# Order of products, weight sums and row finishing in the down half of a squared-ReLU MLP

## Chip, cores and metric

The kernel runs on one core of one Trainium2 chip. The metric is the device time of one execution in microseconds (us); three executions of the kernel before were timed and their median is taken. One further execution was recorded by the hardware profiler, and the times of single instructions come from that one.

A core has TensorE (PE, matrix products into the accumulation banks of PSUM), VectorE (DVE), ScalarE (ACT), GpSimd (POOL) and SyncE (SP, which issues most DMAs). Each engine works through its own list of instructions in order.

## What is computed

Two decoder layers on 1024 tokens of width 1024, float32 throughout: a latent attention mixer in layer 0, a gated linear recurrence (HGRN2) in layer 1, and after each of them an MLP.

```python
def sq_relu_mlp(h, w1, w2):
    a = jax.nn.relu(h @ w1)
    return (a * a) @ w2          # w1: 1024 x 4096, w2: 4096 x 1024

# per layer
a = rms_norm(h, norm_gains[layer, 2])
h = h + rms_norm(sq_relu_mlp(a, mlp_w1[layer], mlp_w2[layer]), norm_gains[layer, 3])
```

The change touches the second product, `(a * a) @ w2`, with the norm and the residual sum behind it.

## The kernel before

A float32 matrix is used as two parts, a rounded one and the rest. `split` (L76, L77) makes them: ACT copies the rounded part, DVE subtracts it from the source. `mm3` (L81 to L83) adds three partial products of such parts into one bank of PSUM.

`mlp_down` computes `(a * a) @ w2` by a scheme with seven block products in place of eight. Tokens, the 4096 hidden features and the 1024 outputs are each halved; the result has four blocks c11, c12, c21, c22. The left factors are the seven sums of blocks of activations that the up half has left in DRAM (`hsp[0]` to `hsp[6]`); they have the features on the partitions. The right factors are the blocks b11, b12, b21, b22 of the weights and four sums of them, which are made here on DVE from blocks that SP loads into tiles `s11`, `s12`, `s21`, `s22` (their digits are left out in the profile: all are `s`).

The features are taken in two passes, c = 0 and c = 1 (`NC = 2`). One pass has four pairs of 128-wide chunks (`qs`). A product goes over the four pairs; for each pair `factors` loads and splits the left part (`sparts`) and the right part (`right(q)`, then `parts`), and 24 matmuls follow, into four banks, one for each of the four 128-token tiles (`banks`). `more=True` goes on adding to what the banks hold. `gather` moves the four banks to SBUF after a product: ACT copies (L1002) at c = 0 where there is nothing to add to, otherwise DVE adds (L1004). The split parts live in five working tiles `w` (one in `G0`, four in `G`), two for each pair; raw loads pass through three staging tiles.

Before, a pass runs so, where X is a set of four banks from pool `PG` and Y one from `PM`:

- product 0 in X, gathered to `U`; product 1 added to it, gathered to c11
- product 4 in Y with t1 = b12 - b11 (L939, in place in `s11`), gathered to c22; product 2 with b22 added to it, gathered to c12; beside it `less22` (L1018) makes b21 - b22 in `s21`
- product 5 in X with t2 = b22 - t1 (L948, in a tile `s12`), added to `U` (so U holds products 0 and 5 of both passes in the end)
- at c = 1: for each of the first four token tiles c12 += U (L1029), `finish_rows`, c22 += U (L1031), U += c21 (L1032)
- product 6 in Y with t3 = b22 - b12 (L953, after a second load of b12), added to c22; product 3 with t4 (L957, the fifth sum) added to the same banks; at c = 0 copied to c21, at c = 1 added to U by `done`

`finish_rows` takes a finished tile of 128 rows: mean squares on ACT (L135), `rstd` on DVE and a power on POOL (L145), a multiplication by the gains `gpost` on 1024 columns (L199), a fused multiply-add with the residual rows `xt` (L200), a store by POOL, and in layer 0 a second norm for the next mixer (L204). `xt` is one tile in layer 0 and three in layer 1. The last four token tiles are finished by `done`, called from `by_tiles`, which goes through product 3 tile by tile: in layer 0 the last two pairs, in layer 1 all four, whose right parts have tiles of their own there (`wx`). Their residual rows come by `rows_in` into tiles that the weight sums no longer need. In layer 0 the finished rows are transposed on PE (`into_features`, L176) for the next mixer.

What runs when: the program is put in order ahead of time. A planner simulates the engines and on each of them takes, among the instructions that it holds to be ready, the one that stands first in the program. `keep_in_program_order` holds an instruction behind the one that was written just before it for the same engine; the weight sums on DVE and the weight loads on SP have it.

## Time and profile before

| what | us |
|---|---|
| median of 3 runs | 2400.32 |
| lowest and highest | 2399.58, 2401.26 |
| the profiled execution, device time | 2396.59 |
| its span | 2394.9 |
| ACT busy | 1170.9 |
| POOL busy | 355.5 |
| PE's mean granted clock | 0.987 |

Down stage of layer 0: about 830 to 1150 us in the span; of layer 1: about 2065 us to the end. In rows of the timeline the first number is the start and the second the duration; `x2` is two instructions merged, and brackets show how long the engine stood idle before and what ended that. In rows by stretch each engine has its busy time and its count of instructions; PEclk is the granted clock as a share of full speed. A matmul's recorded duration is longer than the step from one to the next, since they are pipelined.

### The profile page before, as it was taken

Reading aid. Unit: us, or ns where it says so; the run is one execution under the profiler, and the core shown is the slowest. Engines: PE = TensorE matmul, PEld = TensorE weight load, DVE = VectorE, ACT = ScalarE, POOL = GpSimd, SP = SyncE. Lnnn points to the kernel's source line nnn. Section 1 sums busy time; section 2 is a strip of 40 time slices with the busy share of each in tenths; the row PEclk is TensorE's granted clock in tenths of the full one; section 3 lists DMA queues with packets and bytes.
Section 4 is the critical chain, followed back from the end, with each engine's and each line's share of the span. In section 5 each row is a group of like instructions: output and inputs, shape, how many; then the busy total and the mean of one; then the engine's idle time right before and its main releaser. Section 6 shows DMA issues by size and latency. Waiting matters only on the chain. (4 is left out here: it accounts for less than half of the span.)

```text
span 2394.9 us, 30791 instructions
## 1 busy us (share of the span) xinstructions
PE 2285.7 (95%) x11487; PEld 1918.8 (80%) x11487; DVE 1616.4 (67%) x2311; ACT 1170.9 (49%) x1908; POOL 355.5 (15%) x718
## 2 busy tenths in 40 slices
PE   9999999988899999998899999999978999999996
PEld 8889998866688878886788888888766788888885
DVE  5657884477676557578765667756777767467578
ACT  5445654363344454433575546754453445443443
POOL 1300000121121200001332213221211212100002
PEclk9999999999999999999999999999999999999998
DMA  6000002485554584554612333222455545663743
GB/s 216 27 27 10 10 10 90 157 267 164 172 184 151 187 299 133 190 181 149 219 45 88 106 105 116 83 77 80 150 184 187 200 149 172 214 238 132 257 138 141
DMA packets 229540, 341.51 MB, mean 143 GB/s; under 512 B 16999, under 2 KB 136846, under 8 KB 229390
## 3 DMA queue, kind: packets, MB, share of 16 engines
q1 hardware_dynamic: 205582, 259.84, 33.7%
q0 software_dynamic: 23808, 79.71, 9.0%
q8 instruction: 90, 1.47, 0.3%
q14 instruction: 60, 0.49, 0.1%
HBM read 255.61 MB, written 83.89 MB: 142 GB/s over the span
## 5 line engine op out<-in xcount | busy, mean ns | idle before, releaser
L77 DVE TENSOR_TENSOR w<-raw,w 128x1024 fp32r<-128x1024 f32 (+1 forms) x256 | 280.7, 1102 | 175.9 <-ACT w L76 174.9
L76 ACT ACTIVATE w<-raw 128x1024 fp32r<-128x1024 f32 (+1 forms) x256 | 240.7, 947 | 248.0 <-PE mm L83 82.1
L81 PE MATMUL mm<-A,w 128*128 128x512 f32 x832 | 330.9, 400 | 30.5 <-ACT he L784 12.8
L82 PE MATMUL mm<-A,w 128*128 128x512 f32 x832 | 329.7, 397 | 0.6 <-DVE A L77 0.5
L83 PE MATMUL mm<-A,w 128*128 128x512 f32 x832 | 327.9, 396 | 0.5 <-DVE w L77 0.5
L76 ACT ACTIVATE w<-s 128x1024 fp32r<-128x1024 f32 x156 | 165.1, 1058 | 318.6 <-PE c L83 107.0
L77 DVE TENSOR_TENSOR w<-s,w 128x1024 fp32r<-128x1024 f32 x156 | 190.6, 1222 | 143.2 <-ACT w L76 142.7
L81 PEld LDWEIGHTS mm<-A,w 128*128 128x128 f32 x832 | 158.4, 191 | 72.5 <-ACT he L784 16.1
L145 POOL TENSOR_TENSOR rstd<-rstd,nhalf 128x1 f32<-128x1 f32 x56 | 56.3, 1008 | 964.9 <-DVE rstd L144 939.0
L83 PEld LDWEIGHTS mm<-A,w 128*128 128x128 f32 x832 | 158.7, 191 | 34.2 <-DVE w L77 1.0
L82 PEld LDWEIGHTS mm<-A,w 128*128 128x128 f32 x832 | 158.4, 190 | 33.0 <-DVE A L77 1.4
L82 PE MATMUL mm<-w,w 128*128 128x512 f32 x432 | 171.0, 396 | 12.2 <-DVE w L77 12.2
L781 POOL DMA_DIRECT2D hsp<-h x208 | 112.1, 540 | 467.2 <-ACT h L785 242.6
L83 PE MATMUL mm<-w,w 128*128 128x512 f32 x432 | 169.6, 394 | 0.0
L81 PE MATMUL mm<-w,w 128*128 128x512 f32 x432 | 154.9, 394 | 4.1 <-DVE y L1004 3.2
L81 PE MATMUL mm<-w,A 128*128 128x256 f32 (+2 forms) x352 | 111.1, 318 | 3.6 <-ACT A L76 3.4
L784 ACT ACTIVATE h<-h 128x512 f32<-128x512 f32 x96 | 60.2, 627 | 109.2 <-DVE h L825 70.9
L83 PE MATMUL mm<-w,A 128*128 128x256 f32 (+2 forms) x352 | 111.0, 317 | 0.0
L82 PE MATMUL mm<-w,A 128*128 128x256 f32 (+2 forms) x352 | 110.7, 316 | 0.0
L82 PEld LDWEIGHTS mm<-w,w 128*128 128x128 f32 x432 | 82.1, 190 | 31.2 <-DVE w L77 14.3
L81 PEld LDWEIGHTS mm<-w,w 128*128 128x128 f32 x432 | 81.4, 189 | 24.8 <-ACT w L76 5.7
L81 PE MATMUL c<-T,w 128*128 128x512 f32 x256 | 99.7, 390 | 1.6 <-DVE h L825 1.6
(415 smaller groups left out, 5705.0 us busy)
## 6 DMA issues: line engine op xcount, KB each, us to landing
raw<-in_mlp_w_dram SPq DMA_DIRECT2D x108, 512.0 KB, 4.2
hsp<-h POOLq DMA_DIRECT2D x208, 256.0 KB, 3.1
s<-in_mlp_w_dram SPq DMA_DIRECT2D x80, 512.0 KB, 5.5
raw<-hsp SPq DMA_DIRECT2D x76, 512.0 KB, 4.1
raw<-in_hgrn_w_in_dram SPq DMA_DIRECT2D x64, 512.0 KB, 4.1
sx<-hsp SPq DMA_DIRECT2D x36, 512.0 KB, 4.2
res<-xt POOLq DMA_DIRECT2D x20, 512.0 KB, 4.1
xt<-in_x_dram SPq DMA_DIRECT2D x16, 512.0 KB, 5.7
```

Of the source, the lines that this page charges most:

```text
L76: ACT.activation(dst[:, 0], src, AF.Copy)
L77: DVE.tensor_tensor(dst[:, 1], src, dst[:, 0].bitcast(F32), ALU.subtract)
L81: PE.matmul(ps, lhs[0], rhs[0], start=start, stop=False, skip_group_check=more)
L82: PE.matmul(ps, lhs[0], rhs[1], start=False, stop=False, skip_group_check=more)
L83: PE.matmul(ps, lhs[1], rhs[0], start=False, stop=stop, skip_group_check=more)
L145: POOL.tensor_tensor(r, r, nhalf[:, :1], ALU.pow)
L781: POOL.dma_start(hsp[i, p * P:(p + 1) * P, :], h)
L784: ACT.activation(h, src, AF.Relu)
```

## The change

- The sums are made in place, four for each pair: t1 as before; after product 2's factors `sums` makes t2 in `s11` and t4 in `s21` from it; t3 is made in `s22` beside product 5.
- At c = 1 `U` (product 0 of both passes) is added to c12, c22 and c21 right after product 1. The mean squares of c11 and the gains' multiplication of that half follow there; `finish_rows` gets the other half as `part` and its residual rows by `rows_in` in `s11` tiles.
- Products 5, 6 and 3 accumulate in one set of banks X: after product 5 it is added to c12, after 6 to c22, after 3 to c21. The two sets change pools at odd c.

```diff
-    def finish_rows(wp, y, ms, gpost, gpre, src, dst, t, xt_bufs=2, xt=None):
+    def finish_rows(wp, y, ms, gpost, gpre, src, dst, t, xt_bufs=2, xt=None, part=slice(0, D)):
...
-        DVE.tensor_tensor(y, y, gpost, ALU.mult)
+        DVE.tensor_tensor(y[:, part], y[:, part], gpost[:, part], ALU.mult)
...
-                def t2(q):
-                    t = new(wr, [P, 2, 512], F32, "s12", 3)
-                    tc.keep_in_program_order(DVE.tensor_tensor(t, s22[q], s11[q], ALU.subtract))
-                    return t
+                def sums(q):
+                    tc.keep_in_program_order(DVE.tensor_tensor(s11[q], s22[q], s11[q], ALU.subtract))
+                    tc.keep_in_program_order(DVE.tensor_tensor(s21[q], s21[q], s11[q], ALU.subtract))
                 def t3(q):
                     b12 = load12(q)
-                    tc.keep_in_program_order(DVE.tensor_tensor(b12, s22[q], b12, ALU.subtract))
-                    return b12
-                def t4(q):
-                    tc.keep_in_program_order(DVE.tensor_tensor(s21[q], s21[q], s11[q], ALU.add))
-                    return s21[q]
+                    tc.keep_in_program_order(DVE.tensor_tensor(s22[q], s22[q], b12, ALU.subtract))
...
+                first, second = [(PG, "mm"), (PG, "tr")], [(PM, "mm"), (PM, "c")]
+                if c % 2:
+                    first, second = second, first
+                X = four(*first)
                 product(0, X, first11)
                 gather(U, X)
                 product(1, X, load21, True)
                 gather(c11, X)
+                if last:
+                    for to in (c12, c22, c21):
+                        for t in range(4):
+                            DVE.tensor_tensor(to[t], to[t], U[t], ALU.add)
+                    gpost = row_bcast(wp, "gpost", norm_gains[layer, 3], D)
+                    ms11 = []
+                    for t in range(4):
+                        ms11.append(meansq(c11[t], new(wp, [P, 512], BF16, "junk"), new(wp, [P, 1], F32, f"ms{t}")))
+                        DVE.tensor_tensor(c11[t], c11[t], gpost[:, :512], ALU.mult)
+                Y = four(*second)
                 product(4, Y, t1)
                 gather(c22, Y)
-                def less22(q):
-                    tc.keep_in_program_order(DVE.tensor_tensor(s21[q], s21[q], s22[q], ALU.subtract))
-                product(2, Y, load22, True, less22)
+                product(2, Y, load22, True, sums)
                 gather(c12, Y)
-                X = four((PG, "mm"), (PG, "tr"))
-                product(5, X, t2)
-                gather(U, X, U)
+                X = four(*first)
+                product(5, X, s11.get, after=t3)
+                gather(c12, X, c12)
                 if last:
                     for t in range(4):
-                        DVE.tensor_tensor(c12[t], c12[t], U[t], ALU.add)
-                        finish_rows(wp, y[t], None, gpost, gpre, src, dst, t, xt_bufs=1 if gpre is not None else 3)
-                        DVE.tensor_tensor(c22[t], c22[t], U[t], ALU.add)
-                        DVE.tensor_tensor(U[t], U[t], c21[t], ALU.add)
-                Y = four((PM, "mm"), (PM, "c"))
-                product(6, Y, t3)
-                gather(c22, Y, c22)
+                        ms12 = meansq(c12[t], new(wp, [P, 512], BF16, "junk"))
+                        finish_rows(wp, y[t], [ms11[t], ms12], gpost, gpre, src, dst, t, xt=rows_in("s11", t),
+                                    part=slice(512, D))
+                product(6, X, s22.get, True)
+                gather(c22, X, c22)
                 if not last:
-                    product(3, Y, t4, True)
-                    gather(c21, Y)
+                    product(3, X, s21.get, True)
+                    gather(c21, X)
```

Behind this, `done` adds X to c21 in place of Y to U, and `by_tiles` takes `s21.get` and loads its residual rows into `s21` tiles.

More of the change, by code (lines that the diff above doesn't have):

```diff
@@ L997, in mlp_down, with rows_in @@
                     y += [new(wp, [P, D], F32, f"y{t}") for t in range(4, NT)]
+                def rows_in(tag, t):
+                    xt = new(wp, [P, 2, 512], F32, tag, KC // 2).rearrange("p a b -> p (a b)")
+                    tc.keep_in_program_order(SP.dma_start(xt, src[t * P:(t + 1) * P, :]))
+                    return xt
                 def gather(out, banks, base=None):
@@ L1033, in mlp_down @@
-                Y = four((PM, "mm"), (PM, "c"))
-                product(6, Y, t3)
-                gather(c22, Y, c22)
-                def rows_in(t):
-                    xt = new(wp, [P, 2, 512], F32, "s11", KC // 2).rearrange("p a b -> p (a b)")
-                    tc.keep_in_program_order(SP.dma_start(xt, src[t * P:(t + 1) * P, :]))
-                    return xt
+                        ms12 = meansq(c12[t], new(wp, [P, 512], BF16, "junk"))
+                        finish_rows(wp, y[t], [ms11[t], ms12], gpost, gpre, src, dst, t, xt=rows_in("s11", t),
+                                    part=slice(512, D))
@@ L1053, in done @@
                     def done(t):
-                        DVE.tensor_tensor(c21[t], Y[t], U[t], ALU.add)
+                        DVE.tensor_tensor(c21[t], X[t], c21[t], ALU.add)
                         finish_rows(wp, y[4 + t], None, gpost, gpre, src, dst, 4 + t, xt=xts[t])
                         POOL.dma_start(later[t * P:(t + 1) * P, :], y[4 + t])
-                    product(3, Y, t4, True, n1=2)
+                    product(3, X, s21.get, True, n1=2)
                     xts = []
-                    by_tiles(3, Y, t4, 2, done, False, lambda: xts.extend(rows_in(4 + t) for t in range(4)))
+                    by_tiles(3, X, s21.get, 2, done, False, lambda: xts.extend(rows_in("s21", 4 + t) for t in range(4)))
                 else:
@@ L1070, in done @@
                         xt = xts[t]
[L1071 removed]
+                        DVE.tensor_tensor(c21[t], X[t], c21[t], ALU.add)
                         ms = meansq(c21[t], new(wp, [P, 512], BF16, "junk"))
```

5 lines of the change are left out of this document (1 added, 4 removed).

## The prediction

> **What bounds the kernel now.** I read the page's busy line first, then busy time by stretch for each product of the down stage, then PE's timeline where the stretches are not full, and at last VectorE's own order there.
>
> ```profile
> PE 2285.7 (95%) x11487; PEld 1918.8 (80%) x11487; DVE 1616.4 (67%) x2311; ACT 1170.9 (49%) x1908; POOL 355.5 (15%) x718
> ```
>
> TensorE sets the time: it is busy for 95% of the span. An edit on VectorE (DVE) is worth something only where PE waits for DVE. A product of the down stage is 96 matmuls (4 pairs of weight chunks x 2 x 4 banks x 3 partial products), in the order 0, 1, 4, 2, 5, 6, 3, once for c = 0 and once for c = 1. These rows are layer 0, c = 1, products 1, 4, 2, 5, the first 21.8 us of 6 and its rest; then layer 1, the same two parts of 6.
>
> ```profile
> core 0: us, PE busy (x) PEld busy (x) DVE busy (x) ACT busy (x) POOL busy (x), PEclk, DMA share, GB/s
> 1005.20:1027.00 21.80, 21.80 (x98) 18.05 (x97) 13.25 (x13) 8.04 (x9) 0.00 (x0) 1.00 0.84 305
> 1027.00:1048.80 21.80, 21.80 (x97) 17.80 (x96) 15.19 (x16) 8.74 (x11) 0.00 (x0) 1.00 0.47 164
> 1048.80:1070.60 21.80, 21.80 (x97) 18.05 (x98) 16.87 (x17) 7.95 (x8) 0.00 (x0) 1.00 0.39 125
> 1070.60:1092.30 21.70, 21.70 (x98) 17.96 (x97) 16.62 (x18) 8.04 (x8) 0.00 (x0) 1.00 0.55 191
> 1092.30:1114.10 21.80, 17.00 (x67) 13.29 (x66) 21.34 (x27) 9.35 (x14) 7.21 (x2) 0.92 0.20 73
> 1114.10:1125.10 11.00, 7.86 (x39) 6.38 (x38) 8.26 (x11) 4.91 (x8) 2.57 (x3) 1.00 0.47 143
> 2328.20:2350.00 21.80, 15.63 (x61) 12.21 (x60) 21.80 (x31) 10.14 (x19) 8.53 (x5) 0.88 0.19 65
> 2350.00:2361.20 11.20, 9.53 (x38) 7.12 (x37) 11.20 (x12) 3.92 (x4) 1.60 (x3) 0.93 0.72 254
> ```
>
> Products 1 to 5 keep PE full, with DVE busy 13 to 17 of 21.8 us. In product 6 it turns over: DVE has no idle time (21.80 of 21.80) and PE drops to 15.63. So the last two products of c = 1 are bound by DVE, twice in the kernel, and nothing else of the down stage is. How much is lost there:
>
> ```profile
> 1086.82 0.62 PE L81 MATMUL mm<-w,w 128*128 128x512 f32 x2
> 1092.26 0.62 PE L81 MATMUL mm<-w,w 128*128 128x512 f32 x2
> 1109.29 0.80 PE L82 MATMUL mm<-w,w 128*128 128x512 f32 x1 [4.73 <-DVE w L77]
> 1120.92 1.03 PE L176 MATMUL tr<-ident,y 128*128 128x128 f32 x8
> 1125.13 0.47 PE L81 MATMUL mm<-w,w 128*128 128x512 f32 x1 [3.17 <-DVE y L1004]
> 1150.24 0.40 PE L83 MATMUL c<-w,w 128*128 128x512 f32 x1
> ...
> 2328.19 0.61 PE L81 MATMUL mm<-w,w 128*128 128x512 f32 x2
> 2346.61 0.80 PE L82 MATMUL mm<-w,w 128*128 128x512 f32 x1 [6.00 <-DVE w L77]
> 2347.21 0.63 PE L83 MATMUL mm<-w,w 128*128 128x512 f32 x1
> 2347.64 0.63 PE L82 MATMUL mm<-w,w 128*128 128x512 f32 x1
> 2355.88 0.50 PE L82 MATMUL mm<-w,w 128*128 128x512 f32 x1 [1.21 <-DVE w L77]
> 2361.17 0.47 PE L81 MATMUL mm<-wx,w 128*128 128x512 f32 x1 [0.46 <-DVE y L1004]
> 2382.83 0.39 PE L83 MATMUL c<-wx,w 128*128 128x512 f32 x1
> ```
>
> The first two rows are the starts of two neighbouring pairs of chunks: 24 matmuls in 5.44 us, 0.227 each, so 21.8 a product and 43.5 for products 6 and 3. Layer 1 takes from 2328.19 to 2383.06 (the last start plus one step), 54.9: **11.4 us lost**. Layer 0 takes from 1092.26 to 1150.47, 58.2, with three groups of 8 transposes in it (1.03 each): **11.6 us lost**. The waits are only part: after the 6.00 us wait matmuls step by 0.43 (2347.21 to 2347.64), the lower clock that PEclk 0.88 shows. With the waits this goes too.
>
> **What DVE does there.** Layer 1's group rows for 2328.2 to 2350, then single rows in order of time:
>
> ```profile
> L199 DVE TENSOR_TENSOR y<-y,gpost 128x1024 f32<-128x1024 f32 x4 | 4.9, 1215 | 0.0
> L1029 DVE TENSOR_TENSOR y<-y,u 128x512 f32<-128x512 f32 x4 | 2.7, 682 | 0.0
> ...
> 2327.50 1.28 DVE L1004 TENSOR_TENSOR u<-mm,u 128x512 f32<-128x512 f32 x2
> 2328.70 1.28 DVE L1004 TENSOR_TENSOR u<-tr,u 128x512 f32<-128x512 f32 x2
> 2344.21 1.21 DVE L199 TENSOR_TENSOR y<-y,gpost 128x1024 f32<-128x1024 f32 x1
> 2345.35 1.21 DVE L77 TENSOR_TENSOR w<-s,w 128x1024 fp32r<-128x1024 f32 x1
> ```
>
> Back to back, a 512-wide operation costs 0.60 us (two in 1.20) and a 1024-wide one 1.14. The split at 2345.35, the one that PE's 6.00 us wait ends on, stands behind 16 adds of 512 (four each at L1004, L1029, L1031, L1032) and four full multiplications (L199).
>
> **The change, summed for DVE.** Per product: 8 splits, 9.1; a set of 4 gathers, 2.4; 4 weight sums, 4.6.
>
> - Product 6 before: 9.1 + 2.4 + 12 adds (7.2) + 4.6 (t3) + per row a multiplication 1.14 and a fused step 1.2 (9.4) = 32.7, and a second fused step per row in layer 0 (4.8) = 37.5. Room: 21.8.
> - Product 6 after: the adds are in product 1, t3 is in product 5, half of each multiplication is in product 4. Left: 9.1 + 2.4 + 4 x (0.6 + 1.2) = 18.7; layer 0 23.5.
> - Product 3: 9.1 + 2.4 + 4.6 becomes 11.5; t4 is now made in product 2.
> - Product 1 gets 7.2 on 13.25, 20.4. Product 4 gets 2.4 on 15.19, 17.6. Product 2 gets a second sum, 4.6 on 16.87, 21.4. Product 5 has t3 where t2 was, 16.6.
>
> All of them fit but layer 0's product 6, 1.7 over, which the slack ahead of and behind it takes up. The five working weight tiles hold a product's split about one pair (5.44 us) ahead, which covers the fullest, product 2. If that cover is gone, a wait like layer 1's is the price, 11 us with its clock. I take 1 us for products 1 to 2 of both layers (0 to 22), and 2 us left in product 6 (0 to 11.6).
>
> The sums removed at c = 0 (one in five) are worth nothing there: PE had no wait in those products. Moved DMAs: `load12` goes from product 6 to 5 (DMA share 0.55, room), and the rows of `src` come through SP into `s11` tiles, behind the splits of product 5, which run a pair ahead of PE; behind them on SP stand the loads of product 6's left factors, whose tiles come free at the same pace. Below nothing, since layer 0's single `xt` tile goes: inside the 11.6. ACT has 8 to 10 of 21.8 in each stretch, so four earlier mean squares are free.
>
> **The new wait.** Product 6 must now accumulate in the banks that product 5's gather is still reading, four boundaries more (two layers, c = 0 and 1); PE's stream stands behind it. The nearest rows are the 6 to 3 boundary at c = 0, where this is so already, and all waits of this kind in the run:
>
> ```profile
> 960.99 0.39 PE L83 MATMUL c<-w,w 128*128 128x512 f32 x1
> 961.36 0.47 PE L81 MATMUL mm<-w,w 128*128 128x512 f32 x1
> ...
> PE mm L81 <- DVE y L1004: 3.6, 2, 3.2
> ```
>
> A step of 0.37 in place of 0.227: 0.14 lost. The two recorded waits (3.2 and 0.46) are those where DVE had a queue. I take 0.14 x 4 = 0.6 (up to 3.2 each, 12.8); the gather is ahead of product 6's splits in priority. A rule speaks against this edit: the Trainium skill, "Perfetto Trace Analysis", section "Matmuls", wants independent groups of matmuls rotated through different PSUM banks, so that an eviction overlaps the next group. By it the sum would carry four whole sets of gathers, 9.6 in place of 0.6. The row above does not bear it out where DVE is free: four banks in turn leave each gather some 2 us.
>
> **The first power on POOL.**
>
> ```profile
> 2339.02 7.95 POOL L145 TENSOR_TENSOR rstd<-rstd,nhalf 128x1 f32<-128x1 f32 x4 [262.21 <-DVE rstd L144]
> ```
>
> Four take 7.95 after 262 us of idle. It delays the fused steps to about 8 us into product 6, before and after; splits stand between them now as then. Cost 0, up to 5 if DVE's stream is blocked behind it.
>
> **The end of the span, and what follows layer 0.** Three rows of DVE at the end of layer 1, one of ACT after layer 0, and two waits of PE there:
>
> ```profile
> 2384.40 0.69 DVE L1071 TENSOR_TENSOR y<-c,u 128x512 f32<-128x512 f32 x1
> 2387.65 0.69 DVE L1073 TENSOR_TENSOR y<-y,gpost 128x512 f32<-128x512 f32 x1
> 2389.13 1.41 DVE L1077 SCALAR_TENSOR_TENSOR s<-y,rstd,s 128x512 f32<-128x512 f32 x2 [0.73 <-POOL rstd L145]
> ...
> 1189.54 1.06 ACT L76 ACTIVATE w<-raw 128x1024 fp32r<-128x1024 f32 x1 [4.70 <-DMA raw<-in_hgrn_w_in_dram]
> ...
> PE mm L81 <- ACT f L1122: 4.3, 1, 4.3
> PE mm L81 <- ACT A L76: 1.1, 1, 1.1
> ```
>
> The last row's multiplication waits from 2384.40 to 2387.65 behind other rows, because late sums (t4) made PE go by pairs, not by tiles, and three tiles ended together. With the sums ready the tiles end apart: up to 3.2 saved, I take 2 (0 to 3.2). After layer 0, PE waits 1.1 for the first rows' features, which now come earlier: I take 1 (0 to 1.1). The 4.3 us wait further on hangs on a load of the next mixer's weights (ACT's row at 1189.54, 4.70 for the DMA); I leave it, and keep 4 us either way for the range.
>
> **Sum.** -11.6 - 11.4 - 2 - 1 + 2 + 1 + 0.6 = -22.4. The profiled execution took 2396.59 (span 2394.9 and 1.7 around it), which gives 2374.2. It lies 3.7 under the median of the runs, 2400.32; I set the saving against the median and say **2378**.
>
> **Rivals.**
>
> - A, half: finishing work has priority over product 6's splits, and layer 0 is still 1.7 over; the order puts row steps ahead of the third pair's splits, and one wait of about 5 us with its slow clock stays in each layer. For it: 16 operations went ahead of a needed split before. Against: they are 8 short ones now. 2378 + 2 x 5.5 = 2389. Chance 0.20.
> - B, the banks: each of the four new boundaries costs its whole gather, 2.4, as in the rule above: 2378 + 9 = 2387. For: the 3.2 us wait. Against: the 0.14. Chance 0.06.
> - C, slower: DVE's queue moves to products 1 to 2 of c = 1, 59.4 of 65.4 us full. It decides once the work ahead of a needed split there passes 5.44 us: then each layer waits there as now in product 6 (11.5), and product 5's gather comes late behind it (3.2 and as much for the clock, 6.4 in all) while product 6's wait stays halved: +11.5 + 6.4 - 6 is 12 a layer on 2400.32, 2424. Chance 0.06.
> - D, it does not do what it says: the planner's order keeps the same operations ahead of the splits, or the next mixer's wait gives the gain back; within 0.2%, 2396 to 2405. Chance 0.08.
>
> The forecast has 0.60 (2371 to 2385). A measurement of this kernel tells about 0.2%, 5 us, from no change. Faster is forecast, A and B: 0.86; same 0.08; slower 0.06. The range, 2370 (all waits, 3.2, 1.1 and some of the 4.3 gone) to 2391 (A with 2 more), holds 0.86 by the cases, somewhat less at its ends.
>
> **What would show it.** Right: in both layers product 6 of c = 1 takes some 22 to 24 us at PEclk 1.00, DVE has idle time there, no split ends a PE wait over 1 us, products 1, 4 and 2 show DVE near 20 and PE full, and 5 to 6 steps by under 0.5. Wrong: a wait on L77 in product 6 (A), on L1004 at 5 to 6 (B), PE gaps in 1 to 2 (C), or as many lost microseconds behind the down stage as were won in it (D).

## The result and the profile after

| | us |
|---|---|
| predicted | 2378, range 2370 to 2391 |
| after, median of 4 runs | 2372.7 (2370.5 to 2374.67) |
| before, beside them, median of 4 | 2400.79 (2399.58 to 2405.72) |
| ratio, 95% interval | 0.9879 [0.9862, 0.9896] |
| after once more, in a second set of runs, median of 5 | 2375.27, ratio 0.9905 [0.9888, 0.9921] |
| the profiled execution of after | 2374.67, span 2373.0 (before 2396.59, span 2394.9) |

In this section the two profiled executions are compared, whose spans differ by 21.9 us. The milestones are starts of PE's matmuls in the timeline: the start of each layer's down stage, the start of product 6 at c = 1, the end of product 3 (last start plus one step of 0.23), the end of the span. The down stage of layer 1 starts at 2052.6 us in before and at 2045.6 in after.

| part, us | before | after | difference |
|---|---|---|---|
| up to the down stage of layer 0 | 826.1 | 828.0 | +1.9 |
| from there to product 6, c = 1 | 266.2 | 265.9 | -0.3 |
| products 6 and 3, layer 0 | 58.2 | 47.9 | **-10.3** |
| from there to the down stage of layer 1 | 902.1 | 903.8 | +1.7 |
| from there to product 6, c = 1 | 275.6 | 274.9 | -0.7 |
| products 6 and 3, layer 1 | 54.9 | 43.5 | **-11.4** |
| from there to the end | 11.8 | 9.0 | -2.8 |

The page's busy line shows PE with nearly the same work in a shorter span:

```profile
PE 2284.0 (96%) x11487; PEld 1923.2 (81%) x11487; DVE 1599.9 (67%) x2303; ACT 1171.8 (49%) x1909; POOL 344.2 (15%) x718
```

Busy time by stretch of after, columns as in the prediction. First layer 0, c = 1, products 1, 4, 2, 5, 6, 3 (six rows); then the same six products of layer 1.

```profile
1006.80:1028.50 21.70, 21.70 (x98) 17.96 (x97) 19.94 (x25) 7.94 (x8) 0.00 (x0) 1.00 0.70 252
1028.50:1050.30 21.80, 21.80 (x97) 17.85 (x96) 17.56 (x20) 10.91 (x17) 0.00 (x0) 1.00 0.75 253
1050.30:1072.10 21.80, 21.80 (x97) 17.87 (x97) 20.59 (x21) 7.96 (x8) 0.00 (x0) 1.00 0.57 192
1072.10:1093.80 21.70, 21.70 (x97) 17.98 (x96) 16.23 (x17) 8.77 (x10) 0.00 (x0) 1.00 0.64 199
1093.80:1118.00 24.20, 23.77 (x114) 19.59 (x112) 23.29 (x32) 16.74 (x26) 7.55 (x11) 1.00 0.42 149
1118.00:1141.80 23.80, 23.80 (x113) 19.64 (x114) 15.85 (x21) 10.29 (x17) 1.84 (x2) 1.00 0.48 155
...
2233.40:2255.20 21.80, 21.80 (x98) 18.06 (x97) 20.04 (x25) 8.04 (x9) 0.00 (x0) 1.00 0.71 254
2255.20:2276.90 21.70, 21.70 (x97) 17.75 (x96) 17.46 (x20) 10.82 (x17) 0.00 (x0) 1.00 0.70 246
2276.90:2298.70 21.80, 21.80 (x96) 17.88 (x97) 21.80 (x21) 12.04 (x12) 0.00 (x0) 1.00 0.50 169
2298.70:2320.50 21.80, 21.80 (x98) 18.04 (x97) 19.28 (x21) 9.15 (x11) 0.00 (x0) 1.00 0.67 223
2320.50:2342.20 21.70, 21.70 (x97) 18.00 (x96) 18.10 (x24) 9.65 (x16) 6.63 (x8) 1.00 0.54 187
2342.20:2364.00 21.80, 21.80 (x97) 17.84 (x96) 13.97 (x23) 5.98 (x14) 1.66 (x3) 1.00 0.38 149
```

PE is full in all of them, at clock 1.00, but for 0.43 us in layer 0. Layer 1's product 6 went from 15.63 of 21.8 at clock 0.88 to 21.70 of 21.70, and DVE has 3.6 us idle in it. Most of what layer 0 has over 21.8 there (24.2 and 23.8) is no loss: PE makes 32 transposes in between, some 0.13 us each (8 in 1.03); in before 24 of them stood in this stretch and 8 behind it.

PE's waits in the down stage, first all of layer 1's, then all of layer 0's (us in total, times, longest):

```profile
PE mm L81 <- ACT u L1006: 0.2, 1, 0.2
...
PE mm L81 <- ACT w L76: 0.5, 1, 0.5
PE mm L81 <- DVE y L1008: 0.4, 1, 0.4
PE mm L82 <- DVE w L77: 0.2, 1, 0.2
```

Of the waits for a split in product 6 (6.00 and 4.73 us before) nothing is left. The new wait for the banks is next, from PE's timeline: the last matmul of product 5 and the first of product 6 in layer 1, then the first of product 3 in layer 0 behind a group of transposes.

```profile
2320.25 0.39 PE L83 MATMUL c<-w,w 128*128 128x512 f32 x1
2320.48 0.39 PE L81 MATMUL mm<-w,w 128*128 128x512 f32 x1
...
1117.99 0.47 PE L81 MATMUL mm<-w,w 128*128 128x512 f32 x1 [0.43 <-DVE y L1008]
```

2320.25 to 2320.48 is the ordinary step, 0.23. The other three boundaries from 5 to 6 step by 0.23 as well. DVE's timeline shows why there is room: two gathers merged from 2318.64, the third from 2320.00, the fourth only from 2321.27, with a row step between them.

```profile
2318.64 1.37 DVE L1008 TENSOR_TENSOR y<-mm,y 128x512 f32<-128x512 f32 x2
2320.00 0.69 DVE L1008 TENSOR_TENSOR y<-c,y 128x512 f32<-128x512 f32 x1
...
2320.67 0.68 DVE L200 TENSOR_TENSOR y<-y,gpost 128x512 f32<-128x512 f32 x1
2321.27 0.68 DVE L1008 TENSOR_TENSOR y<-c,y 128x512 f32<-128x512 f32 x1
```

A gather of a bank has to be done only when PE comes to that bank again, and PE takes the four banks one after the other. The first bank's gather starts at 2318.64 while PE is still in the last two.

And the tail in layer 1, the last row's steps on DVE:

```profile
2364.20 0.69 DVE L1075 TENSOR_TENSOR y<-c,y 128x512 f32<-128x512 f32 x1 [0.56 <-PE c L83]
2365.74 0.69 DVE L1077 TENSOR_TENSOR y<-y,gpost 128x512 f32<-128x512 f32 x1 [0.85 <-ACT junk L135]
2367.22 1.41 DVE L1081 SCALAR_TENSOR_TENSOR s<-y,rstd,s 128x512 f32<-128x512 f32 x2 [0.73 <-POOL rstd L145]
```

From the add to the multiplication it takes 1.54 us now, 3.25 before: the row no longer stands behind others, and what is left of the idle time is its own chain (the mean square on ACT, the power on POOL). That is 1.7 of the 2.8 us. The other 1.1 lie ahead of the add: it starts 0.2 us behind the end of product 3 (2364.00) now and started 1.35 us behind it before (2383.05 to 2384.40).

### The profile page after: what moved, and what is told of

Read it like the earlier page. It is cut to its first block, busy times and chain, and to the rows that moved or that the text cites. A ratio compares the mean times of both kernels' runs of the same rounds, so it can differ in the third digit from the quotient of the medians.

```text
span 2373.0 us, 30769 instructions
## 1 busy us (share of the span) xinstructions
PE 2284.0 (96%) x11487; PEld 1923.2 (81%) x11487; DVE 1599.9 (67%) x2303; ACT 1171.8 (49%) x1909; POOL 344.2 (15%) x718
## 5 line engine op out<-in xcount | busy, mean ns | idle before, releaser
L145 POOL TENSOR_TENSOR rstd<-rstd,nhalf 128x1 f32<-128x1 f32 x56 | 45.1, 807 | 965.6 <-DVE rstd L144 942.2
L81 PE MATMUL c<-T,w 128*128 128x512 f32 x256 | 99.7, 390 | 1.5 <-DVE h L827 1.5
L82 PE MATMUL c<-T,w 128*128 128x512 f32 x256 | 99.6, 389 | 0.0
L83 PE MATMUL c<-T,w 128*128 128x512 f32 x256 | 98.8, 389 | 0.0
```

The source lines that it names most:

```text
L81: PE.matmul(ps, lhs[0], rhs[0], start=start, stop=False, skip_group_check=more)
L82: PE.matmul(ps, lhs[0], rhs[1], start=False, stop=False, skip_group_check=more)
L83: PE.matmul(ps, lhs[1], rhs[0], start=False, stop=stop, skip_group_check=more)
L145: POOL.tensor_tensor(r, r, nhalf[:, :1], ALU.pow)
```

## The experiments

Two parts of the change could have taken PE's waits away: the weight sums that are ready earlier, and the adds and multiplications that left product 6. The theory of the prediction is the load: PE waits when DVE has more to do in product 6 than there is room, whatever the work is. The rival is the chain: a weight sum made inside the product that uses it puts a further step on DVE ahead of the rounding on ACT and the split on DVE, and that is late even where there is room for the load. Besides, the banks (rival B), the 7.95 us power on POOL, and what lies between the two down stages had to be tested. For each run "stretch" means products 6 and 3 at c = 1, counted from 96 steps behind the first matmul of product 5, so that a delay within product 5 or at its end is in it too (counted from the first matmul of product 6 it is 0.10 to 0.15 us shorter in adds only, t3 late and idle sum, 2.0 us shorter in layer 1 of adds late, and the same in the others); without any wait it takes 43.5 us in layer 1 (192 steps of 0.2267), and in layer 0 that and some 0.13 us for each transpose in it.

| kernel | median, us (runs) | ratio to before [interval] | stretch, layer 0 (transposes in it) | between the down stages | stretch, layer 1 | tail |
|---|---|---|---|---|---|---|
| before | | 1 | 58.2 (24) | 902.1 | 54.9 | 11.8 |
| after | 2372.7 (4) | 0.9879 [0.9862, 0.9896] | 47.9 (32) | 903.8 | 43.5 | 9.0 |
| sums only | 2378.88 (4) | 0.9914 [0.9896, 0.9931] | 46.5 (16) | 902.2 | 48.4 | 9.0 |
| adds only | 2373.21 (4) | 0.9891 [0.9876, 0.9906] | 46.9 (24) | 896.2 | 47.7 | 11.1 |
| adds late | 2379.15 (4) | 0.9917 [0.9902, 0.9933] | 47.7 (32) | 907.1 | 45.5 | 8.9 |
| gain late | 2364.46 (4) | 0.9851 [0.9835, 0.9868] | 47.1 (32) | 894.6 | 43.5 | 8.9 |
| own banks | 2366.89 (1) | | 49.3 (32) | 894.4 | 45.0 | 9.0 |
| power before | 2400.26 (1) | | 58.0 (24) | 901.7 | 55.7 | 11.8 |
| t3 late | 2376.03 (1) | | 48.7 (32) | 895.2 | 48.3 | 8.9 |
| idle sum | 2369.9 (1) | | 47.0 (28) | 898.9 | 43.7 | 9.0 |

Sums only, adds only, adds late and gain late stood beside 7 runs of before, median 2399.58 (2394.74 to 2402.43); the last four beside one, 2402.95. The stretches are read from the one profiled execution of each. Where a kernel was profiled twice, in the second set of runs below, they agree within 0.05 us.

**Sums only.** The kernel before, with the four sums in place and at their new times, everything else as it was.

```diff
-                product(2, Y, load22, True, less22)
+                product(2, Y, load22, True, sums)
...
-                product(5, X, t2)
+                product(5, X, s11.get, after=t3)
...
-                product(6, Y, t3)
+                product(6, Y, s22.get)
...
-                    product(3, Y, t4, True)
+                    product(3, Y, s21.get, True)
```

> The kernel before with the weight sums alone taken from the change (t2, t4 and t3 made in place, ahead); U, the adds, the row finishing and the two sets of banks stay as before. Stretch = first matmul of product 6 at c = 1 to the end of the last of product 3: before 54.9 us in layer 1 and 58.2 in layer 0, after the change 43.5 and 48.0. Theory 1 (the load of VectorE in product 6 sets the loss: work there less the 21.8 us of the product): 4.6 us of sums leave product 6, so layer 1 keeps 28.1 of work, some 6 us of loss, a stretch near 50; layer 0 loses some 7, a stretch near 53. Time some 10 us under the kernel before. Theory 2 (the chain load, sum, split inside products 6 and 3 was the delay, not the load): without the chain both stretches fall to within 2 us of the changed kernel's, and the time to some 20 us under before.

In layer 0 nearly the whole loss is gone (46.5 is 43.5, 2.1 for 16 transposes and 0.9), in layer 1 11.4 became 4.9. So layer 1 came out near what theory 1 says (50) and layer 0 near what theory 2 says; theory 1 had it at 53. The groups of DVE in layer 1's product 6 (busy us, mean ns of one, idle before):

```profile
L199 DVE TENSOR_TENSOR y<-y,gpost 128x1024 f32<-128x1024 f32 x4 | 4.9, 1217 | 0.0
L1024 DVE TENSOR_TENSOR y<-y,u 128x512 f32<-128x512 f32 x4 | 2.8, 688 | 0.0
L1022 DVE TENSOR_TENSOR y<-y,u 128x512 f32<-128x512 f32 x4 | 2.7, 686 | 0.0
L1025 DVE TENSOR_TENSOR u<-u,y 128x512 f32<-128x512 f32 x4 | 2.7, 684 | 0.0
```

And PE's longest wait there:

```profile
2336.49 0.50 PE L82 MATMUL mm<-w,w 128*128 128x512 f32 x1 [1.94 <-DVE w L77]
```

The twelve adds and four whole multiplications are still there (L199, L1022, L1024, L1025: 13.1 us), DVE has no idle time, and makes 6 splits in these 21.8 us, where PE uses up 8. In before it made 5, in after 7 (with time to spare). That is the load, without a late sum. In layer 0 the same 21.8 us hold the twelve adds too, but only two of the multiplications and two of the fused steps, and DVE makes 7 splits there (20.88 us busy): more of the row finishing comes later, into product 3. That its single `xt` tile spreads the rows out is likely, but no run here tests it.

**Adds only.** After, with the old sums at their old times and the old tiles for the residual rows.

```diff
-                product(2, Y, load22, True, sums)
+                product(2, Y, load22, True, less22)
...
-                product(5, X, s11.get, after=t3)
+                product(5, X, t2)
...
-                product(6, X, s22.get, True)
+                product(6, X, t3, True)
...
-                    product(3, X, s21.get, True)
+                    product(3, X, t4, True)
```

> The changed kernel with the five old weight sums in their old places (t3 in product 6, t4 in product 3) and the old residual tiles; the moved adds, the early half of the gains and the one set of banks stay. Theory 1 (load): VectorE has 23.3 us of work in product 6 of layer 1 and 28.1 in layer 0: a loss of some 2 and 3, stretches near 45.5 and 50.5; the last tiles end together again, so the 2.8 us won at the end of the span are lost. Time some 17 us under the kernel before. Theory 2 (the chain of the sums): most of the loss stays, stretches over 50 and 54, time less than 10 us under before.

Layer 0 is almost without a loss (46.9 is 43.5, 3.1 and 0.3), which neither theory had; layer 1 keeps 4.2, between the two theories, and the tail keeps 11.1 of 11.8, so the tail's gain belongs to the sums. Both stretches and the tail, without the transposes, are 121.8 us in before and 96.2 in after: 25.6 saved. Sums only has 101.8 and adds only 102.6, so each half of the change alone saves 20.0 or 19.2. They do not add up, since in layer 0 either one is enough, and in layer 1 each takes more than half. The two medians beside each other would mislead here: adds only (2373.21) looks as good as after (2372.7) because its time between the down stages is 7.6 us shorter, in code that the edit does not touch.

**Adds late, gain late.** After, with the adds of U back behind product 5; and after, with the whole multiplication by the gains in `finish_rows`.

```diff
-                    for to in (c12, c22, c21):
-                        for t in range(4):
-                            DVE.tensor_tensor(to[t], to[t], U[t], ALU.add)
...
+                        DVE.tensor_tensor(c12[t], c12[t], U[t], ALU.add)
                         ms12 = meansq(c12[t], new(wp, [P, 512], BF16, "junk"))
...
+                        for to in (c22, c21):
+                            DVE.tensor_tensor(to[t], to[t], U[t], ALU.add)
```

> The changed kernel with the twelve adds of U put back behind product 5, where they stand among the row steps. Theory 1 (load): 7.2 us more in product 6, 25.9 of 21.8 in layer 1 and 30.7 in layer 0: a loss of some 4 and 5, waits of TensorE on a split in product 6, stretches near 47.5 and 53; the time some 9 us over the changed kernel's. Theory 2 (the chain of the sums): no loss, within 2 us of the changed kernel. Theory 3 (what counts is whether 16 operations stand in one block ahead of the needed split, not the sum): more than theory 1, near 8 in each layer.

```diff
-                        DVE.tensor_tensor(c11[t], c11[t], gpost[:, :512], ALU.mult)
...
-                                    part=slice(512, D))
+                                    part=slice(0, D))
```

> The changed kernel with the whole multiplication by the gains back in the row finishing (the mean squares of c11 stay early). Theory 1 (load): 2.4 us more in product 6, 21.1 of 21.8 in layer 1, which fits, so nothing; 25.9 in layer 0, of which some 4 can go over into product 3 as before the change: 0 to 2 us. Time within 2 us of the changed kernel's. If the loss started at a lower fill than 21.8, layer 1 would show it here first, with 1 to 3 us.

The edit of adds late moved less than it says. The adds to c22 and c21 (L1043) need nothing of product 5, so the planner put eight of the twelve well ahead of it: in layer 1 four from 2236.37 to 2240.50, at the start of product 1, and four from 2283.24 to 2289.58, in product 2. Only the four adds to c12 come with product 6, from 2325.88 on: 2.4 us in place of 7.2. The row of product 5 of layer 1, then that of product 6; then one of the adds in product 2, a split in product 5, and PE's wait:

```profile
2302.70:2326.40 23.70, 22.03 (x97) 17.94 (x96) 21.41 (x23) 8.06 (x9) 0.00 (x0) 1.00 0.62 207
2326.40:2348.20 21.80, 21.80 (x97) 17.94 (x97) 20.50 (x28) 10.89 (x18) 5.07 (x8) 1.00 0.50 186
```

```profile
2283.24 0.69 DVE L1043 TENSOR_TENSOR y<-y,u 128x512 f32<-128x512 f32 x1
...
2305.53 1.23 DVE L77 TENSOR_TENSOR wx<-s,wx 128x1024 fp32r<-128x1024 f32 x1
2310.89 0.50 PE L82 MATMUL mm<-w,w 128*128 128x512 f32 x1 [1.67 <-DVE w L77]
```

Product 6 is full, with DVE busy 20.50 of 21.8 us; the 25.9 of theory 1 were not reached, so this run tests neither theory 1 nor theory 3. What is lost, 2.0 us, is lost in product 5 (23.7 us; from the first matmul of product 6 at 2326.44 the stretch is 43.5). The wait stands behind splits into `wx`: these are product 3's right parts, which have tiles of their own in layer 1, so the planner may make them as soon as their sum is there. In after they stand at 2282.86, 2288.53 and 2294.21, in product 2, and at 2301.68 in product 5, some 40 to 60 us before product 3 needs them, and there they cost nothing. In adds late the four adds to c22 are in product 2 besides, DVE is full there (21.80 of 21.80), and two of the four splits into `wx` come in product 5, at 2305.53 and 2308.46, ahead of the split that PE waits for. Layer 0, without such tiles, loses at most the 0.43 us in either run. So four adds in product 6 cost nothing, and four in product 2 go with a loss of 2.0 us, by what they displaced as DVE's order reads; no run moves these four alone, and all twelve stand beside product 6 only in before and in sums only. The median of adds late is higher by more, because it has 907.1 us between the down stages. The early half of the multiplication is worth nothing in the stretch: gain late has 43.5 and 47.1. Why its median is lower by 8 us is the last experiment.

**t3 late, idle sum.** The load against the chain, with the same work in product 6. In the first, t3 is made in place as `right` of product 6; in the second t3 stays beside product 5, and product 6 gets a sum of the same size that nobody reads.

```diff
-                product(5, X, s11.get, after=t3)
+                product(5, X, s11.get)
...
-                product(6, X, s22.get, True)
+                product(6, X, t3, True)
```

> The changed kernel with t3 alone back in product 6: load, sum and split there, ahead of TensorE. 4.6 us more on VectorE in product 6, in the chain of the split. Theory 1 (load alone): as e8, a loss of 0 to 1.5 us in layer 1, stretch 43.5 to 45. Theory 2 (the chain): more than e8 by 2 us or more, as with the sums all late in e2 (47.7).

```diff
-                product(6, X, s22.get, True)
+                def idle_sum(q):
+                    w = new(wr, [P, 2, 512], F32, "s12", 3)
+                    tc.keep_in_program_order(DVE.tensor_tensor(w, s21[q], s21[q], ALU.add))
+
+                product(6, X, s22.get, True, idle_sum)
```

> The changed kernel with one more 1024-wide add on VectorE for each pair of product 6, whose result nothing uses: the load of e7 without its chain. Theory 1 (load alone): 23.3 us in product 6 of layer 1, a loss of 0 to 1.5 us, stretch 43.5 to 45, the same as e7. Theory 2 (the chain): nothing here, 43.5.

48.3 against 43.7 in layer 1, as theory 2 says: four sums (4.6 us) for the pairs of product 6 in both, and those whose result is needed there cost 4.8 us and the others 0.2. In layer 0 it is less: t3 late has 48.7 with 32 transposes against the 47.9 of after. Each is read from one execution. The row of the stretch with the idle sum, then of t3 late DVE's and ACT's rows ahead of PE's wait, and the wait; between them two of ACT's rows with the idle sum:

```profile
2315.50:2337.30 21.80, 21.80 (x97) 18.00 (x97) 21.80 (x28) 10.43 (x17) 5.08 (x8) 1.00 0.47 171
```

```profile
2326.76 1.06 ACT L76 ACTIVATE w<-s 128x1024 fp32r<-128x1024 f32 x1 [2.75 <-PE c L83]
2327.73 1.04 ACT L76 ACTIVATE w<-raw 128x1024 fp32r<-128x1024 f32 x1
```

```profile
2328.38 2.47 DVE L201 SCALAR_TENSOR_TENSOR s<-y,rstd,s 128x1024 f32<-128x1024 f32 x2
...
2331.91 1.21 DVE L956 TENSOR_TENSOR s<-s,s 128x1024 f32<-128x1024 f32 x1
2333.81 1.06 ACT L76 ACTIVATE w<-raw 128x1024 fp32r<-128x1024 f32 x1 [4.38 <-PE c L83]
2334.77 1.04 ACT L76 ACTIVATE w<-s 128x1024 fp32r<-128x1024 f32 x1
2335.86 0.73 PE L81 MATMUL mm<-w,w 128*128 128x512 f32 x2 [2.09 <-ACT w L76]
```

With the idle sum DVE has no idle time at all (21.80 of 21.80), and PE none either; ACT rounds a right part (`s`) and a left part (`raw`) one behind the other, 11 and 12 us into product 6. In t3 late, whose product 6 starts 1.6 us later, three of the four sums are made in time (two of them while PE is still in product 5); the fourth stands at 2331.91 behind two fused steps and a split (DVE has no idle time ahead of it, so it did not wait for b12) and ends at 2333.12. On ACT a left part now stands ahead of that right part and waits until 2333.81 for PE to free a tile, so the right part is rounded only at 2334.77, 18 us into the product. PE waits 2.09 us for it, and then steps by 0.43 for some 3.4 us more. DVE is not even full there: 19.42 of the first 21.8 us. So a full DVE costs nothing by itself while the splits run a pair ahead; a sum inside the product that uses it uses up this lead, by where it stands among the other work and by the order that the planner then gives ACT. Before had both: sums in the chain, and 16 adds and four multiplications ahead of them.

**Own banks.** After, with products 5, 6 and 3 as in the sums, but product 6 begins in the other set of banks, so that it need not wait for product 5's gather; product 5 is added to c22 and c21 too, 8 more gathers (4.8 us of DVE) at c = 1. The two sets no longer change pools at odd c.

```diff
-                if c % 2:
-                    first, second = second, first
...
-                product(6, X, s22.get, True)
+                gather(c22, X, c22)
+                if last:
+                    gather(c21, X, c21)
+                else:
+                    gather(c21, X)
+                X = four(*second)
+                product(6, X, s22.get)
...
-                    gather(c21, X)
+                    gather(c21, X, c21)
```

> The changed kernel with product 5 in a set of banks of its own and 6 and 3 in the other, as before the change; product 5 is then added to c22 and c21 by eight adds more in a pass. The rule that independent groups should change banks would have the changed kernel lose at its four boundaries from 5 to 6, up to 2.4 us each. Theory 1 (load of VectorE): the gathers hide, the changed kernel's stretch of products 6 and 3 in layer 1 is 43.5 us, which is 192 steps with nothing lost; so nothing is won, and 4.8 us more on VectorE in product 6 cost some 1 to 2 us in layer 1 (stretch 44.5 to 45.5) and 0 to 2 in layer 0 (48 to 50). By the rule the passes from product 4 to 6 at c = 0 would shorten by some 2 us each.

The stretches are longer, not shorter: 45.0 against 43.5, 49.3 against 47.9. With 32 transposes in both, that is 1.5 and 1.4 us more, within what theory 1 says. At c = 0 products 4, 2, 5 and 6 take 21.76 us each in both kernels, so nothing is won there either. The shared banks cost nothing that a second set could give back; the additional gathers can account for the rest, since PE now waits 0.78 us for a split in product 6 of layer 1 (0.8 in layer 0), where after has no such wait. Its lower total comes from between the down stages (894.4).

**Power before.** The kernel before, with one more mean square and power, unused, ahead of product 5, to see whether 260 us of idle time make POOL's first power slow.

```diff
+                if last:
+                    warm = rstd_from(meansq(c11[0], new(wp, [P, 512], BF16, "junk")))
```

> The kernel before with one mean square and one power on POOL, whose result nothing uses, ahead of product 5 at c = 1. The first power in product 6 took 6.62 us (layer 0) before and 0.88 after the change, both after over 250 us of idle. If POOL's idleness makes it long, the added power is the long one, and the one in product 6 falls under 1 us. If VectorE's unbroken run of operations on two SBUF tensors holds POOL off, the added power is short (VectorE has gaps in product 5) and the one in product 6 still takes 6 to 8 us, ending half a microsecond after that run's end. Stretches as before, 58.2 and 54.9, within 1 us.

POOL's rows of layer 0 (the added power, then the first real one); then the first two powers of layer 1 in after, and DVE's row beside the second:

```profile
1036.10 0.56 POOL L145 TENSOR_TENSOR rstd<-rstd,nhalf 128x1 f32<-128x1 f32 x1 [198.20 <-DVE rstd L142]
1106.94 6.61 POOL L145 TENSOR_TENSOR rstd<-rstd,nhalf 128x1 f32<-128x1 f32 x1 [70.28 <-DVE rstd L144]
```

```profile
2320.91 0.88 POOL L145 TENSOR_TENSOR rstd<-rstd,nhalf 128x1 f32<-128x1 f32 x1 [251.24 <-DVE rstd L144]
2322.17 0.86 POOL L145 TENSOR_TENSOR rstd<-rstd,nhalf 128x1 f32<-128x1 f32 x1 [0.38 <-DVE rstd L144]
...
2322.54 1.28 DVE L201 SCALAR_TENSOR_TENSOR s<-y,rstd,s 128x1024 f32<-128x1024 f32 x1
```

So idle time is not the cause: 0.56 us after 198 us of it, 6.61 after 70, 0.88 after 251. In layer 1 the four powers again take 7.95 together. What differs is DVE. The slow one ends with DVE's unbroken run, here its last row and the first after the gap:

```profile
1111.93 1.22 DVE L77 TENSOR_TENSOR w<-s,w 128x1024 fp32r<-128x1024 f32 x1
1113.59 1.28 DVE L200 SCALAR_TENSOR_TENSOR xt<-y,rstd,xt 128x1024 f32<-128x1024 f32 x1 [0.44 <-POOL rstd L145]
```

From 1106.94, where the power starts, to 1113.15 DVE runs TENSOR_TENSORs with two inputs in SBUF back to back, and the power ends at 1113.55, 0.4 us behind the last of them. In after the first power starts beside such an operation too (L200 at 2320.67 above, to 2321.35) and ends 0.43 us behind it, at 2321.79; a gather, which reads a bank of PSUM, follows there (L1008 at 2321.27). The second ends 0.4 us behind an L200 that ends at 2322.63, and what follows there is L201, a SCALAR_TENSOR_TENSOR that also has two inputs in SBUF. So two inputs alone do not tell which run holds a power off. The Trainium skill, "SBUF — State Buffer", section "Who interferes with whom", says that a DVE instruction with two SBUF inputs and a GpSimd instruction that reads SBUF exclude each other, and that whoever comes first keeps the other out for the whole instruction. That fits the two powers of after. In power before the power waited for a whole run of TENSOR_TENSORs, not for one. No run separates this further, so the cause is argued from these times and not shown.

**Gain late in one layer, and both kernels again.** Gain late was 8 us faster than after, with the same stretch in layer 1 and one 0.8 us shorter in layer 0. Nearly all of its gain lies between the two down stages (894.6 against 903.8), where the code is the same. Either that is the order in which the planner put that code behind the changed layer 0 (theory P), or the first run was lucky (Q), or the edit itself is worth something. So the edit was made in one layer only, by a condition on `gpre_row`, which is None in layer 1.

```diff
-                        DVE.tensor_tensor(c11[t], c11[t], gpost[:, :512], ALU.mult)
+                        if not (gpre_row is None):
+                            DVE.tensor_tensor(c11[t], c11[t], gpost[:, :512], ALU.mult)
...
-                                    part=slice(512, D))
+                                    part=slice(0, D) if gpre_row is None else slice(512, D))
```

This is the one for layer 1; the other has the condition turned round.

> The changed kernel once more, on one chip beside the kernel before and the three runs that follow. Expected 2368 to 2375 us, a ratio of 0.987 to 0.990. Its time between the end of layer 0's down part and the start of layer 1's is about 904 us, as in its first trace, since the program is the same; if it is not, this part varies from run to run and not with the program.

> The changed kernel with the gain multiplied late, once more. Theory P (the gain over the changed kernel lies in the order in which the planner puts unchanged work between the two down parts): 2361 to 2367 us, about 895 us between the down parts, stretches of products 6 and 3 as in the changed kernel within 1 us. Theory Q (the first run was a lucky one): equal to the changed kernel within 0.2%.

> The gain is multiplied late in layer 1 alone; layer 0 is the changed kernel's. Theory P: layer 1's down part stands after the work in question, so about 904 us between the down parts and 2369 to 2376 us, like the changed kernel. If the edit itself (four multiplications less in product 1, four longer ones in product 6) were worth something, half of the gain of 9 us should be seen: 2364 to 2368 us.

> The gain is multiplied late in layer 0 alone. Theory P: the order of the work behind layer 0's down part is that of the kernel with both late, so about 895 us between the down parts and 2361 to 2367 us, the whole gain. If the edit itself counts: half of the gain, 2364 to 2370 us, with the time between the down parts unchanged at 904 us.

All on one chip, beside 9 runs of before with a median of 2398.61 (2393.03 to 2401.06):

| kernel | median, us (runs) | ratio to before [interval] | between the down stages |
|---|---|---|---|
| after | 2375.27 (5) | 0.9905 [0.9888, 0.9921] | 903.8 |
| gain late | 2364.12 (4) | 0.9861 [0.9846, 0.9877] | 895.1 |
| gain late in layer 1 only | 2375.83 (4) | 0.9910 [0.9893, 0.9926] | 902.1 |
| gain late in layer 0 only | 2364.26 (4) | 0.9861 [0.9846, 0.9877] | 894.3 |

Theory P stands on all four; after itself (2375.27, 0.9905) came out just above its forecast. The edit in layer 1 brings nothing, the edit in layer 0 all 11 us, and the same program has the same time there, to 0.5 us, in both sets of runs. The traces show the order itself: between the down stages the instructions of PE, DVE, ACT and POOL come in one and the same sequence in both executions of after and in gain late in layer 1 only, and in one other sequence in both executions of gain late and in layer 0 only. With the first sequence the time there was 902.1 to 903.8, with the second 894.3 to 895.1. (Adds late has nearly the first one, with differences from 645 us on, and took 907.1.) Where the time is: the row by stretch for the first part of the next mixer and PE's longest wait in it, both of after; then that row and the same step of gain late in layer 0 only.

```profile
1143.00:1400.00 257.00, 243.70 (x1431) 212.33 (x1430) 157.43 (x225) 146.16 (x251) 66.95 (x160) 0.95 0.35 105
```

```profile
1298.41 2.08 PE L1222 MATMUL c<-qq,kr 128*128 128x128 f32 x8 [3.56 <-DVE qq L1173]
```

```profile
1143.00:1400.00 257.00, 247.01 (x1497) 213.82 (x1496) 165.51 (x238) 149.74 (x256) 73.65 (x170) 0.99 0.34 104
```

```profile
1289.68 1.16 PE L1223 MATMUL c<-qq,kr 128*128 128x128 f32 x8 [1.30 <-DVE qq L1174]
```

In after PE gets through 66 recorded matmuls less in 257 us, at a granted clock of 0.95 instead of 0.99, and waits 3.56 us instead of 1.30 for the same step (3.32 in the second execution of after, 1.28 in that of gain late). Of the 66 some six belong to the windows, which begin 1.2 and 3.8 us behind the end of the down stage; the first 258.2 us behind that end hold 1436 and 1496. The clock does not account for all of it: before has 0.99 in the 258.2 us behind its down stage, and 902.1 us in all. What in the plan of layer 0 moves that step was not followed. Gain late, in layer 0 alone or in both layers, is the fastest version of this study, 1.4% below before; the reason is the order it happens to give the next mixer, not the multiplication.

## Why the prediction came out

The time, 2372.7 and 2375.3 us, lies within the range and 3 to 5 us below the 2378 predicted; faster was right. Step by step, on the profiled executions, whose difference was predicted as -22.4 and is -21.9:

- **What bounds.** Right. PE was held by DVE in products 6 and 3 of c = 1, and nowhere else in the down stage by more than 0.3 us; PE's waits for splits there are gone.
- **-11.4 in layer 1, -11.6 in layer 0.** Layer 1 gave 11.4. Layer 0 gave 10.3; 1.0 of the rest is 8 transposes that moved into its stretch, and 0.43 us of wait is left from 6 to 3.
- **+2 left in product 6.** Too much: 0 in layer 1, 0.4 in layer 0. DVE's own sums there were good for after: 18.7 predicted and 18.10 measured in layer 1, 23.5 and 23.29 in layer 0. How they were read was too coarse. Idle sum fills DVE for 21.8 us without a cost, t3 late costs 4.8 us with 19.42 of 21.8. And the sum gave layer 0 the greater load before, 37.5 against 32.7; sums only, which takes 4.6 off both, leaves a loss of 0.9 in layer 0 and of 4.9 in layer 1. The load alone does not decide; the place of a sum in its product's chain does too, and the prediction had no term for it. It came out all the same, since the change takes away both.
- **+1 in products 1 to 2.** It was 0.1: products 1, 4 and 2 of c = 1 take 65.6 us in after and 65.5 in before, over both layers 0.1 more. From the start of the down stage to product 6 after is even 1.0 shorter over both layers; half of that stands in products 6 and 3 of c = 0, to which the prediction gave no worth. Products 1 and 4 had the predicted load (20.4 and 17.6; measured 19.94 and 17.56 in layer 0). Products 2 and 5 of layer 1 had more than the predicted 21.4 and 16.6 (21.80 and 19.28): the sums that are ready early let product 3's splits into `wx` move up there, which the prediction did not see. There it cost nothing; in adds late it cost 2.0.
- **+0.6 for the banks.** 0.00 at four boundaries, and own banks found nothing to win. Rival B did not happen: four banks in turn give each gather its time. The rule of the Trainium skill, "Perfetto Trace Analysis", section "Matmuls", that it quoted, speaks of different banks for successive groups; that it would need a second set of four, as the prediction read it, is not borne out here.
- **-2 in the tail.** -2.8. The bound of 3.2 was not that of the wait it named: from the add to the multiplication 1.54 of 3.25 us stay, so 1.7 were won there, and the other 1.1 ahead of the add, of which the prediction does not speak.
- **The power on POOL.** Its cost of nothing was right, but "before and after" was wrong: 0.88 us in after. The first fused step stands at 2322.54, 2.1 us into product 6, where 8 were expected; in before it stands at 2346.48, 18.3 us into it, so 8 was not right for before either.
- **-1 and ±4 behind layer 0.** Wrong in size. The time between the down stages went up by 1.7, and over the kernels of this study it lies between 894.3 and 907.1 us in unchanged code. ±4 was too narrow. By luck it did not show, because this edit came out near the place of before.
- **From the saving to the time.** The 3.7 us by which the profiled execution of before lay under its median were added to the forecast; the profiled execution of after lay 2.0 above its own first median. Over 9 runs the one program of after spread from 2370.5 to 2377.3, before over its 21 timed runs from 2393.0 to 2405.7, so this correction was of the size of the spread. Without it the forecast is 2374.2, within 1.5 us of both medians.

Rivals A, C and D did not happen: no split ends a wait in products 6 and 3, PE is full in products 1 to 2, and nothing was given back behind the stage but 1.7 us. What C feared, a full DVE in product 2 that makes a later split late, can be seen in adds late.

## What to carry to other kernels

When an engine is full, ask of each of its instructions whether somebody waits for its result in the same stretch. Work that only fills it was free here up to its last idle microsecond; sums made in the product that uses them cost 4.8 us, through the one that came late. Look in the trace where moved work went: of twelve adds put late in the program the planner put eight early. Compare edits by the stretch that they touch, not by the total alone: with an order that is planned anew for each program, unchanged code behind it moved by up to 13 us, half of what this change was worth.

## What was not expected of the hardware

- A power on 128 x 1 numbers on POOL took 0.56 to 0.88 us, and 6.61 while DVE ran TENSOR_TENSORs on two SBUF tensors without a gap (the four of layer 1 took 7.95 in all); it ended some 0.4 us behind the last of them, and 198 or 251 us of idle time ahead of it made no difference.
- Executions of one program spread by 0.3% to 0.5%, so the difference of two single profiled executions (21.9 us) and that of the medians (28.1, and 23.3 in the second set) need not agree.
- The granted clock in the next mixer over 257 us was 0.95, 0.97 and 0.97 in three executions of the one order of the same work, and 0.99 in all three of the other.
- A short wait can double its price. In adds only PE's wait of 1.89 us was followed by some 3.4 us of steps of 0.43 in place of 0.227, as in t3 late after 2.09; in sums only a wait of 1.94 was followed by ordinary steps at once.

Adds only, then sums only, behind the wait:

```profile
2334.43 0.63 PE L82 MATMUL mm<-w,w 128*128 128x512 f32 x1
2334.85 0.63 PE L83 MATMUL mm<-w,w 128*128 128x512 f32 x1
```

```profile
2337.07 0.40 PE L82 MATMUL mm<-w,w 128*128 128x512 f32 x1
2337.31 0.40 PE L83 MATMUL mm<-w,w 128*128 128x512 f32 x1
```

The Trainium skill, "TensorE: Matmul & The Clock Gate", section "What's actually happening", has the clock fall after an idle window of some 3.4 us, in windows that run freely. That the windows run freely would explain why equal waits end differently; but waits shorter than a window were enough here, so by these runs a window need not be idle throughout.
